# First pair of blocks loaded singly, x by tokens loaded last, and another rate for loads in the order's model

## The chip, the cores and the metric

One core of one Trainium2 chip runs the kernel. The metric is the device time of one execution in microseconds (us). TensorE (PE) multiplies, VectorE (DVE), ScalarE (ACT) and GpSimd (POOL) work on tiles, and SyncE (SP) issues nearly all DMAs, in one queue.

## The reference

Two decoder layers on 512 tokens of width 1024, f32. `concat` is over the two mixers.

```python
def hybrid_layer(h, p_i, layer_idx, norm_gain, w_in, w_out, ...):
    u = rmsnorm(h, norm_gain) @ w_in
    qa, ka, va, ga, qd, kd, vd, gd = jnp.split(u, list(np.cumsum(IN_SPLITS)[:-1]), axis=-1)
    ...
    y = jnp.concatenate([oa * jax.nn.silu(ga), od * jax.nn.silu(gd)], axis=-1) @ w_out
    h = h + y
    gate = jax.nn.sigmoid(rmsnorm(h, ple_norm_gain) @ w_ple_gate)
    return h + (p_i @ w_ple) * gate
```

`oa` is a dilated window attention over 8 heads, `od` a differential attention over 4 heads. A last RMSNorm follows.

## The kernel before

**Products.** Each f32 operand is split into a high part, rounded to fp32r by ACT, and a low part, the rest, made by DVE or POOL. A product is three passes over the same block of 128 rows of depth: high by high, high by low weights, low by high weights (`PASSES`). Weights come in pairs of blocks of 128x512 (512 KB): one DMA fills a staging buffer (`stg`, or `of` for the fourth pair), ACT writes the high part of both blocks into `ring`, DVE and POOL write the low part of one block each. `ring` has five places for pairs. The input x comes transposed (`xt`, four DMAs of two blocks of 128 channels) into `fr`; ACT and DVE split it with the norm's gain (`gt`) into `xy`.

**The start.** PE first runs `NWARM` matmuls on zeros into one bank (`b<-pt`). The first chunk of products (the values `vd` of layer 0) is made by rows: `units_by_rows` goes over four pairs r of blocks of depth, and for each over the four token tiles t, six matmuls each (two blocks, three passes), into four banks `b_79` to `b_82`. So 96 matmuls of 128x512 stand there (`b<-ring,xy`), and behind them the next chunk's (`b<-xy,ring`). The norm's factor is not in these products; it is applied when a bank is emptied. It comes from x by tokens (`x2`, four DMAs of 512 KB into `fr` and `of`): ACT and DVE sum squares (`x_sumsq`), DVE adds (`rstd`), and POOL takes a power for each of four token tiles (`st<-st 128x1`). `spread` then makes PE transpose the four factors (`b<-idt,st`), ACT copies the result to `cr`, and DVE multiplies the rotary tables by it.

**What sets the order.** Nothing is issued as the code stands. Every operation is recorded with a due place (`plan.at`, `plan.pe`, helper `st`), and `Machine.schedule` replays the records through a model of the engines with a duration for each (`cost`), the loads in one stream at a rate in bytes per us, with at most eight loads in flight; what could run first by this model, and among those what is wanted first, stands first in its engine's order. The chip's engines then each keep that order. All recorded instructions come from one line, 292 (`replay`), so they are told apart by their tiles.

The due places of the first loads:

```python
        st(-8.5, load_gt)
        for r in range(4):
            st(-6 + 0.1 * r, load_xt, r)
        ...
        for t in range(T):
            st(3.0 + 0.3 * t, load_x, t)
            ...
            st(3.2 + 0.3 * t, rstd, t, RS0)
```

Of the kernel before, what the change touches and what calls it, by code (L numbers as in the profile page):

```python
# [11 lines left out]
AF = mybir.ActivationFunctionType  # L12
# [45 lines left out]
class Plan:  # L58
# [7 lines left out]
    def pe(self, t, us, f, *a):  # L66
        self.pieces.append((t, len(self.pieces), us, f, a))

    def at(self, t, us, f, *a):
        self.items.append((t, us, f, a))  # L70
# [16 lines left out]
class Machine:  # L87
# [100 lines left out]
    def schedule(self):  # L188
        log = self.log

        nodes, at_call = [], {}
        for i, x in enumerate(log):
            k = x[6] if x[0] == "PE" else None
            if k is not None and k in at_call:
                nodes[at_call[k]].append(i)
            else:
                if k is not None:
                    at_call[k] = len(nodes)
                nodes.append([i])
        N = len(nodes)  # L200
        eng = [log[n[0]][0] for n in nodes]
        busy, done = [0.0] * N, [None] * N
        for i, n in enumerate(nodes):
            for j in n:
                b, d = self.cost(*log[j][:4])
                done[i] = d if isinstance(d, tuple) else busy[i] + d
                busy[i] += b
        preds, seen = [None] * N, {}
        for i, n in enumerate(nodes):
            dep = set()  # L210
            for j in n:
                todo = self.accesses(log[j])
                for k, m, w in todo:
                    for p, mp, wp in seen.get(k, ()):
                        if (w or wp) and mp & m:
                            dep.add(p)
                for k, m, w in todo:
                    lst = seen.setdefault(k, [])
                    if w:
                        lst[:] = [(p, mp & ~m, wp) for p, mp, wp in lst if mp & ~m]  # L220
                    lst.append((i, m, w))
            dep.discard(i)
            preds[i] = sorted(dep)
        succ = [[] for _ in range(N)]
        for i, ps in enumerate(preds):
            for p in ps:
                succ[p].append(i)

        clock, want = START, [None] * N
        for i in range(N):  # L230
            if eng[i] == "PE":
                want[i] = clock
                clock += busy[i]
        end = clock + 10.0

        def lag(i):
            c = done[i]
            return c[0] + 2.0 + c[1] / 200e3 if isinstance(c, tuple) else c
        for i in range(N - 1, -1, -1):
            w = want[i] if want[i] is not None else end  # L240
            for s in succ[i]:
                w = min(w, want[s] - lag(i) - (MARGIN if eng[s] == "PE" and eng[i] != "PE" else 0.0))
            want[i] = w

        left = [len(p) for p in preds]
        ready_at = [0.0] * N
        free = dict.fromkeys(self.eng, 0.0)
        dma, landed = 0.0, []
        waiting = {e: [] for e in self.eng}
        for i in range(N):  # L250
            if not left[i]:
                waiting[eng[i]].append(i)
        order = []
        for _ in range(N):
            best = None
            for e, lst in waiting.items():
                if not lst:
                    continue
                t = max(free[e], min(ready_at[i] for i in lst))
                if best is None or t < best[0]:  # L260
                    best = (t, e)
            t, e = best
            i = min((i for i in waiting[e] if ready_at[i] <= t + 1e-9), key=lambda i: (want[i], i))
            waiting[e].remove(i)
            order.append((t, len(order), i))
            free[e] = t + busy[i]
            if isinstance(done[i], tuple):

                t = max([t] + landed[-8:-7])
                free[e] = t + busy[i]  # L270
                dma = max(dma, t + 1.4) + done[i][1] / 230e3
                fin = dma + 0.6
                landed.append(fin)
            else:
                fin = t + done[i]
            for s in succ[i]:
                if eng[s] == "PE":

                    r = t + busy[i] if e == "PE" else fin + MARGIN
                else:  # L280
                    r = fin
                ready_at[s] = max(ready_at[s], r)
                left[s] -= 1
                if not left[s]:
                    waiting[eng[s]].append(s)
        self.model = (max(free.values()), order, nodes, eng, busy, preds)
        return [j for _, _, i in order for j in nodes[i]]
# [33 lines left out]
def trunk(tc, x, p, w_in, w_out, w_gate, w_ple, final_gain, tables, xt, gt, lams, sub, out):  # L321
# [4 lines left out]
    ACT, DVE, POOL, SPQ, PE = (M.proxy(e) for e in ("ACT", "DVE", "POOL", "SP", "PE"))  # L326
    mm = PE.matmul

    with tc.tile_pool(name="sb", bufs=1) as sb, tc.tile_pool(name="ps", bufs=1, space=PSUM) as psp, \
# [26 lines left out]
        RS0 = ST[:, 136:140]  # L356
# [5 lines left out]
        FRB = FR.rearrange("p (b n) -> p b n", n=512)  # L362
# [16 lines left out]
        def UT(reg, lo, kb):  # L379
            return XY[reg][:, (8 * lo + kb) * 512:(8 * lo + kb + 1) * 512]  # L380
# [14 lines left out]
        plan = Plan()  # L395
        at, pe = plan.at, plan.pe
        nbank = [0]
        NWARM = 14

        def bank():  # L400
            nbank[0] += 1
            return BANK[2 + (nbank[0] - 1) % 6]
# [10 lines left out]
        def stage(n):  # L413

            return OF[:, 4:6, :] if n == NSTG else STG[:, (n - (n > NSTG)) % NSTG]

        def emit_loads():
            order = sorted(range(len(loads)), key=lambda i: loads[i][:2])
            for n, i in enumerate(order):
                t, us, src, hi, lo, eng = loads[i]  # L420
                st = stage(n)

                def load(st=st, src=src):
                    SPQ.dma_start(st, src)

                def high(st=st, hi=hi):
                    ACT.activation(hi, st, AF.Copy)

                def low(k, st=st, hi=hi, lo=lo, eng=eng):
                    eng[k].tensor_sub(lo[:, k], st[:, k], hi[:, k])  # L430
                if n <= NSTG:
                    at(-10, 54.05 + 0.1 * n, load)
                else:
                    prev = loads[order[n - NSTG - (n < 2 * NSTG + 1)]]
                    at(prev[0], prev[1] + 3.5, load)
                at(t, us, high)
                for k in range(2):
                    at(t, us + 1.0 + 0.5 * k, low, k)
# [42 lines left out]
        def units_by_rows(s0, w, ureg, dones):  # L481
            o = [BANK[0], BANK[1], bank(), bank()]

            def part(r, t):
                for kb in (2 * r, 2 * r + 1):
                    for n, (ul, wl) in enumerate(PASSES):
                        mm(o[t], UT(ureg, ul, kb)[:, t * 128:(t + 1) * 128], w(wl, kb),
                           start=(kb == 0 and n == 0), stop=(kb == KB - 1 and n == 2))
            for r in range(4):
                for t in range(T):  # L490
                    pe(s0 + r + 0.25 * t, 1.362, part, r, t)
            for t in range(T):
                dones[t](s0 + 3.2 + 0.25 * t, o[t])

# [31 lines left out]
        def spread(tt, rs, rot):  # L526
            b = {}

            def tr():
                b[0] = bank()  # L530
                for t in range(T):
                    PE.transpose(b[0][:, t * 128:(t + 1) * 128], rs[:, t:t + 1].to_broadcast([128, 128]), IDT)

            def f():
                ACT.activation(RB, b[0], AF.Copy)
                if rot:
                    DVE.tensor_mul(C0, C, b[0])
                    DVE.tensor_mul(SN0, SN, b[0])
            pe(tt, 0.436, tr)
            at(tt, 0.1, f)  # L540
# [30 lines left out]
            SPQ.dma_start(GT, gt)  # L571

        def load_xt(r):
            SPQ.dma_start(FRB[:, 2 * r:2 * r + 2, :], xt[:, 2 * r:2 * r + 2, :])

        def xt_hi(kb):
            ACT.activation(UT(0, 0, kb), FRB[:, kb, :], AF.Copy, scale=GT[:, kb:kb + 1])
# [20 lines left out]
        def warm_up():  # L598
            b = bank()
            for i in range(NWARM):  # L600
                mm(b, PT[:, 0, 0:128], PT[:, 0, 0:512], start=(i == 0), stop=(i == NWARM - 1))

# [23 lines left out]
        def st(us, f, *a):  # L626
            at(-10, 60 + us, f, *a)
# [3 lines left out]
        for r in range(4):  # L631
            st(-6 + 0.1 * r, load_xt, r)
# [8 lines left out]
        for t in range(T):  # L641
# [1 line left out]
            for h in range(2):  # L643
                st(3.1 + 0.3 * t, x_sumsq, t, h)
            st(3.2 + 0.3 * t, rstd, t, RS0)
        spread(2.5, RS0, True)


        nP = [0]
# [536 lines left out]
```

## Time and profile before

| | |
|---|---|
| median of 3 runs | 687.06 us (686.59 to 687.45) |
| the profiled execution | 686.98 us |
| its span, first to last instruction | 684.9 us |
| PE busy | 673.3 us, 98% |
| DVE, ACT, POOL busy | 435.4, 373.8, 383.4 us |

The span is what the trace shows; 2.1 us of the execution lie outside it. A PE that is busy is not idle, but its matmuls may still be slow: their step is read from the distance of their starts.

### The profile page before, as it was taken

How to read it: one execution, taken by the hardware profiler on the slowest of the kernel's cores; microseconds unless marked ns; L12 is line 12 of the kernel's file. 1: busy time of each engine (PE TensorE's matmuls, PEld its weight loads, DVE VectorE, ACT ScalarE, POOL GpSimd, SP SyncE). 2: the span in 40 equal slices, each digit the busy share in tenths (PEclk: the TensorE clock that was granted, in tenths of full speed). 3: DMA queues.
4: the chain of work that ended last, by engine and by line, in shares of the span. 5: the costliest groups of instructions: out<-in, count | busy, mean ns of one | idle time of the engine just before them, and what ended most of it. 6: DMA issues, size and time to landing. Idle time of an engine off the chain costs nothing.

```text
span 684.9 us, 9572 instructions
## 1 busy us (share of the span) xinstructions
PE 673.3 (98%) x3310; PEld 564.0 (82%) x3310; DVE 435.4 (64%) x839; ACT 373.8 (55%) x782; POOL 383.4 (56%) x289
## 2 busy tenths in 40 slices
PE   9999999999999999999999999999999999999995
PEld 7788888888888888888888888888888888788884
DVE  5447996667766784445443699874777688534333
ACT  6525756558888545425432457663787855453411
POOL 5669460876713357937484867266753246496311
PEclk9999999999999999999999999999999999999998
DMA  8656351435443533434152463233535262343002
GB/s 332 242 155 178 93 153 32 140 107 134 119 118 93 184 123 97 138 106 150 62 175 74 123 177 116 78 107 80 154 96 150 92 217 92 98 149 122 1 32 93
DMA packets 31105, 85.32 MB, mean 125 GB/s; under 512 B 4560, under 2 KB 4816, under 8 KB 31056
## 3 DMA queue, kind: packets, MB, share of 16 engines
q1 hardware_dynamic: 30912, 84.44, 39.9%
q8 instruction: 26, 0.43, 0.2%
q10 hardware_dynamic: 144, 0.26, 0.1%
q14 instruction: 23, 0.19, 0.1%
HBM read 63.72 MB, written 4.19 MB: 99 GB/s over the span
## 4 chain that ended last, share of the span: by engine, by line
PE 94%; DVE 3%; DMA 1%; issue 1%; ACT 0%; POOL 0%; SPq 0%; POOLq 0%; DVEq 0%; ACTq 0%
PE b L292 94%; DVE fr L292 2%; DMA gt<-in_gt_dram 1%; DVE misc L292 1%; DVE xy L292 0%; DVE ring L292 0%; ACT xy L292 0%; POOL st L292 0%; DVE of L292 0%; SPq L292 0%; POOL fr L292 0%; DVE st L292 0%; POOLq L1182 0%; ACT of L292 0%; ACT misc L292 0%
## 5 line engine op out<-in xcount | busy, mean ns | idle before, releaser
L292 PE MATMUL b<-xy,ring 128*128 128x512 f32 x1728 | 419.0, 393 | 0.2
L292 PEld LDWEIGHTS b<-xy,ring 128*128 128x128 f32 x1728 | 318.5, 188 | 63.7 <-DVE fr L292 1.9
L292 POOL TENSOR_TENSOR ring<-stg,ring 128x512 fp32r<-128x512 f32 x164 | 233.8, 1451 | 162.7 <-ACT ring L292 131.9
L292 PE MATMUL b<-ring,xy 128*128 128x512 f32 (+1 forms) x600 | 141.6, 385 | 1.5 <-ACT xy L292 1.3
L292 ACT ACTIVATE ring<-stg 128x1024 fp32r<-128x1024 f32 x95 | 100.0, 1059 | 51.2 <-PE b L292 33.5
L292 PEld LDWEIGHTS b<-ring,xy 128*128 128x128 f32 x600 | 107.4, 188 | 23.3 <-ACT xy L292 1.8
L292 ACT ACTIVATE fr<-fr,st 128x512 f32<-128x512 f32 (+3 forms) x193 | 101.8, 556 | 36.8 <-DVE st L292 34.4
L292 POOL TENSOR_TENSOR fr<-fr 128x512 f32<-128x512 f32 x53 | 74.1, 1400 | 30.1 <-ACT fr L292 25.6
L292 POOL TENSOR_TENSOR fr<-fr,cr 128x512 f32<-128x512 f32 x32 | 43.3, 1352 | 63.4 <-DVE fr L292 63.3
L292 DVE CUSTOM_DVE_ANT_0 fr<-b,ct 128x512 f32<-128x512 f32 (+3 forms) x128 | 58.5, 485 | 31.8 <-PE b L292 31.0
L292 DVE SCALAR_TENSOR_TENSOR xy<-fr,gt,xy 128x512 fp32r<-128x512 f32 x32 | 36.6, 1152 | 30.7 <-ACT xy L292 30.7
L292 PE MATMUL b<-qk 128*128 128x128 f32 (+3 forms) x256 | 52.5, 324 | 0.1
L292 DVE TENSOR_TENSOR ring<-stg,ring 128x512 fp32r<-128x512 f32 x26 | 34.6, 1332 | 22.1 <-ACT ring L292 22.1
L292 DVE TENSOR_TENSOR pt<-b,pt 128x384 fp32r<-128x384 f32 (+1 forms) x72 | 40.2, 593 | 11.9 <-ACT pt L292 11.5
L292 ACT ACTIVATE pt<-b 128x384 fp32r<-128x384 f32 (+1 forms) x72 | 34.6, 525 | 18.3 <-PE b L292 18.1
L292 PEld LDWEIGHTS b<-qk 128*128 128x128 f32 x256 | 38.9, 189 | 4.5 <-issue 0.8
L292 PEld LDWEIGHTS b<-idt,fr 128*128 128x128 f32 x284 | 34.0, 140 | 7.3 <-DVE fr L292 0.8
L292 ACT ACTIVATE nt<-fr 128x512 fp32r<-128x512 f32 x32 | 19.8, 624 | 36.6 <-POOL fr L292 36.6
L292 PE MATMUL b<-idt,fr 128*128 128x128 f32 x284 | 39.7, 272 | 0.0
L292 DVE TENSOR_TENSOR fr<-b,cr 128x512 f32<-128x512 f32 x48 | 32.7, 680 | 10.5 <-PE b L292 10.3
L292 POOL TENSOR_TENSOR st<-st 128x4 f32<-128x4 f32 (+1 forms) x19 | 17.8, 938 | 32.8 <-DVE st L292 32.3
L292 ACT ACTIVATE fr<-fr 128x512 f32<-128x512 f32 x26 | 16.4, 633 | 35.1 <-DVE fr L292 34.5
(78 smaller groups left out, 583.0 us busy)
## 6 DMA issues: line engine op xcount, KB each, us to landing
stg<-in_w_in_dram SPq DMA_DIRECT2D x63, 512.0 KB, 3.4
qk<-nt SPq DMA_DIRECT2D x128, 128.0 KB, 2.3
stg<-in_w_out_dram SPq DMA_DIRECT2D x16, 512.0 KB, 4.2
stg<-in_w_ple_gate_dram SPq DMA_DIRECT2D x16, 512.0 KB, 3.3
fr<-in_xt_dram SPq DMA_DIRECT2D x8, 512.0 KB, 5.2
stg<-in_w_ple_dram SPq DMA_DIRECT2D x4, 512.0 KB, 3.2
hsave<-fr SPq DMA_DIRECT2D x8, 256.0 KB, 2.3
fr<-hsave SPq DMA_DIRECT2D x4, 512.0 KB, 3.8
```

The source lines that it names most:

```text
L292: getattr(self.eng[e], op)(*args, **kw)
```

## The change

The first pair of weight blocks (n = 0) is loaded as two DMAs of 256 KB, and its high part is made in two ACT instructions. The first pair of x's blocks is loaded as two DMAs of 256 KB. On PE the first pair of depth is done block by block over the four token tiles: three matmuls each, twelve for block 0, then twelve for block 1. The warm-up has 11 matmuls for 14. The due place of `spread` moves from 2.5 to 3.3. In the model, loads run at 400e3 bytes per us for 230e3, and a load of at most 65,536 bytes is wanted 6.0 us ahead of its use for 2.0.

```diff
-            return c[0] + 2.0 + c[1] / 200e3 if isinstance(c, tuple) else c
+            if isinstance(c, tuple):
+
+                return c[0] + (2.0 if c[1] > 65536 else 6.0) + c[1] / 200e3
+            return c
...
-                dma = max(dma, t + 1.4) + done[i][1] / 230e3
+                dma = max(dma, t + 1.4) + done[i][1] / 400e3
...
-        NWARM = 14
+        NWARM = 11
...
-                def load(st=st, src=src):
-                    SPQ.dma_start(st, src)
-
-                def high(st=st, hi=hi):
-                    ACT.activation(hi, st, AF.Copy)
+                def load(st=st, src=src, ks=((0, 1) if n == 0 else (slice(0, 2),))):
+                    for k in ks:
+                        SPQ.dma_start(st[:, k], src[:, k])
+
+                def high(st=st, hi=hi, ks=((0, 1) if n == 0 else (slice(0, 2),))):
+                    for k in ks:
+                        ACT.activation(hi[:, k], st[:, k], AF.Copy)
...
-            def part(r, t):
-                for kb in (2 * r, 2 * r + 1):
+            def part(kbs, t):
+                for kb in kbs:
...
-                    pe(s0 + r + 0.25 * t, 1.362, part, r, t)
+                    if s0 == 0 and r == 0:
+                        for k in range(2):
+                            pe(0.5 * k + 0.125 * t, 0.681, part, (k,), t)
+                    else:
+                        pe(s0 + r + 0.25 * t, 1.362, part, (2 * r, 2 * r + 1), t)
...
-            SPQ.dma_start(FRB[:, 2 * r:2 * r + 2, :], xt[:, 2 * r:2 * r + 2, :])
+            for k in ((2 * r,), (2 * r + 1,)) if r == 0 else ((2 * r, 2 * r + 1),):
+                SPQ.dma_start(FRB[:, k[0]:k[-1] + 1, :], xt[:, k[0]:k[-1] + 1, :])
...
-        spread(2.5, RS0, True)
+        spread(3.3, RS0, True)
```

The new rate moves rows on all engines. Three places of the new order follow.

SP's queue from the program's first load on. Before:

```order
L292 DMA stg<-in_w_in_dram 128x1024
L292 DMA fr<-in_xt_dram 128x1024
L292 DMA gt<-in_gt_dram 128x32
L292 DMA stg<-in_w_in_dram 128x1024
L292 DMA fr<-in_xt_dram 128x1024
L292 DMA stg<-in_w_in_dram 128x1024
L292 DMA fr<-in_xt_dram 128x1024
L292 DMA fr<-in_x_dram 128x1024 x2
L292 DMA of<-in_x_dram 128x1024 x2
L292 DMA of<-in_w_in_dram 128x1024
L292 DMA fr<-in_xt_dram 128x1024
L292 DMA stg<-in_w_in_dram 128x1024 x3
```

And now, from the first load on:

```order
L295 DMA gt<-in_gt_dram 128x32
L295 DMA fr<-in_xt_dram 128x512
L295 DMA stg<-in_w_in_dram 128x512 x2
L295 DMA fr<-in_xt_dram 128x512
L295 DMA stg<-in_w_in_dram 128x1024
L295 DMA fr<-in_xt_dram 128x1024
L295 DMA stg<-in_w_in_dram 128x1024
L295 DMA fr<-in_xt_dram 128x1024
L295 DMA of<-in_w_in_dram 128x1024
L295 DMA fr<-in_xt_dram 128x1024
L295 DMA fr<-in_x_dram 128x1024 x2
L295 DMA of<-in_x_dram 128x1024 x2
```

The gains' load went from third to first, the blocks of pair 0 are four loads of 128x512, and x by tokens went behind all of the first chunk's weights and `xt`; the second chunk's first load (`stg<-in_w_in_dram 128x1024 x2`) is the row that follows.

PE and ACT around `spread` (`b_86<-idt,st` on PE, `cr<-b_86` on ACT). Before, on PE from the third pair of depth on, and on ACT from the third pair's split on:

```order
L292 MATMUL b_79<-ring,xy_63 128x512 x6
L292 MATMUL b_80<-ring,xy_63 128x512 x6
L292 MATMUL b_81<-ring,xy_63 128x512 x6
L292 MATMUL b_82<-ring,xy_63 128x512 x6
L292 MATMUL b_86<-idt,st 128x128 x4
L292 MATMUL b_79<-ring,xy_63 128x512 x6
L292 MATMUL b_80<-ring,xy_63 128x512 x6
L292 MATMUL b_81<-ring,xy_63 128x512 x6
L292 MATMUL b_82<-ring,xy_63 128x512 x6
```

```order
L292 ACTIVATE xy_63<-fr,gt 128x512 x2
L292 ACTIVATE fr,st<-fr 128x512 x2
L292 ACTIVATE of,st<-of 128x512 x2
L292 ACTIVATE ring<-of 128x1024
L292 ACTIVATE cr<-b_86 128x512
L292 ACTIVATE xy_63<-fr,gt 128x512 x2
```

And now, the same two places:

```order
L295 MATMUL b_79<-ring,xy_63 128x512 x6
L295 MATMUL b_80<-ring,xy_63 128x512 x6
L295 MATMUL b_81<-ring,xy_63 128x512 x6
L295 MATMUL b_82<-ring,xy_63 128x512 x6
L295 MATMUL b_79<-ring,xy_63 128x512 x6
L295 MATMUL b_80<-ring,xy_63 128x512 x6
L295 MATMUL b_81<-ring,xy_63 128x512 x6
L295 MATMUL b_86<-idt,st 128x128 x4
L295 MATMUL b_82<-ring,xy_63 128x512 x6
```

```order
L295 ACTIVATE ring<-of 128x1024
L295 ACTIVATE xy_63<-fr,gt 128x512 x2
L295 ACTIVATE fr,st<-fr 128x512 x2
L295 ACTIVATE of,st<-of 128x512 x2
L295 ACTIVATE ring<-stg 128x1024 x3
L295 ACTIVATE xy_64<-b_79,st 128x4x128
```

The four transposes went from 72 to 90 of the 96 matmuls, and ACT's split of the last two `xt` blocks no longer stands behind the copy to `cr`, which is five rows further down now.

POOL behind its clearing of `qk`, before and now:

```order
L292 MEMSET qk 64x512 x4
L292 TENSOR_TENSOR ring<-stg,ring 128x512 x3
L292 TENSOR_TENSOR st<-st 128x1 x4
L292 TENSOR_TENSOR ring<-of,ring 128x512
L292 TENSOR_TENSOR ring<-stg,ring 128x512 x9
```

```order
L295 MEMSET qk 64x512 x4
L295 TENSOR_TENSOR ring<-stg,ring 128x512 x3
L295 TENSOR_TENSOR ring<-of,ring 128x512
L295 TENSOR_TENSOR ring<-stg,ring 128x512 x2
L295 TENSOR_TENSOR st<-st 128x1 x4
L295 TENSOR_TENSOR ring<-stg,ring 128x512 x7
```

The four powers stood behind three low parts; now they stand behind six, the last two of which (`x2`) belong to the second chunk's first pair, loaded behind x by tokens.

## Rows read from the trace of the kernel before

**Rows 1.** Page, part 1: busy us, share of the span, instructions.

```profile
PE 673.3 (98%) x3310; PEld 564.0 (82%) x3310; DVE 435.4 (64%) x839; ACT 373.8 (55%) x782; POOL 383.4 (56%) x289
```

**Rows 2.** Chain that ended last, around 25 us: start us, us, what.

```profile
25.14 0.72 ACT xy L292
...
25.89 0.76 DVE xy L292
```

**Rows 3.** Timeline, PE, 0 to 45 us: start, us, what, idle before.

```profile
1.45 6.00 PE L292 MATMUL b<-pt 128*128 128x512 f32 x14 [1.45 <-DVE st L292]
7.28 16.89 PE L292 MATMUL b<-ring,xy 128*128 128x512 f32 x72
24.02 0.60 PE L292 MATMUL b<-idt,st 128*128 128x128 f32 x4
25.91 6.08 PE L292 MATMUL b<-ring,xy 128*128 128x512 f32 x24 [1.29 <-ACT xy L292]
31.82 13.46 PE L292 MATMUL b<-xy,ring 128*128 128x512 f32 x57
```

**Rows 4.** Timeline, PE's weight loads, 0 to 45 us.

```profile
8.03 15.73 PEld L292 LDWEIGHTS b<-ring,xy 128*128 128x128 f32 x70 [0.49 <-DVE xy L292]
...
26.70 4.86 PEld L292 LDWEIGHTS b<-ring,xy 128*128 128x128 f32 x22 [0.49 <-DVE xy L292]
```

**Rows 5.** Timeline, PE: the twelfth and fourteenth warm-up apart, and 8.9 to 23.9 us.

```profile
6.30 0.63 PE L292 MATMUL b<-pt 128*128 128x512 f32 x1
...
7.06 0.39 PE L292 MATMUL b<-pt 128*128 128x512 f32 x1
...
8.60 15.58 PE L292 MATMUL b<-ring,xy 128*128 128x512 f32 x68
```

**Rows 6.** Timeline, ACT, 0 to 45 us.

```profile
4.24 1.06 ACT L292 ACTIVATE ring<-stg 128x1024 fp32r<-128x1024 f32 x1 [2.01 <-DMA stg<-in_w_in_dram]
...
8.01 1.06 ACT L292 ACTIVATE ring<-stg 128x1024 fp32r<-128x1024 f32 x1 [0.20 <-DMA stg<-in_w_in_dram]
9.28 1.34 ACT L292 ACTIVATE xy<-fr,gt 128x512 fp32r<-128x512 f32 x2 [0.21 <-DMA fr<-in_xt_dram]
...
18.24 1.06 ACT L292 ACTIVATE ring<-of 128x1024 fp32r<-128x1024 f32 x1 [0.55 <-DMA of<-in_w_in_dram]
24.65 0.60 ACT L292 ACTIVATE cr<-b 128x512 f32<-128x512 f32 x1 [5.35 <-PE b L292]
```

**Rows 7.** Timeline, DVE and then POOL, 0 to 45 us.

```profile
5.33 0.69 DVE L292 TENSOR_TENSOR ring<-stg,ring 128x512 fp32r<-128x512 f32 x1 [3.92 <-ACT ring L292]
7.23 1.41 DVE L292 SCALAR_TENSOR_TENSOR xy<-fr,gt,xy 128x512 fp32r<-128x512 f32 x2 [1.21 <-ACT xy L292]
...
9.15 1.80 POOL L292 TENSOR_TENSOR ring<-stg,ring 128x512 fp32r<-128x512 f32 x1 [1.99 <-ACT ring L292]
...
16.20 3.33 POOL L292 TENSOR_TENSOR st<-st 128x1 f32<-128x1 f32 x4 [2.89 <-DVE st L292]
...
27.50 7.78 POOL L292 TENSOR_TENSOR ring<-stg,ring 128x512 fp32r<-128x512 f32 x6 [6.32 <-PE b L292]
```

**Rows 8.** Loads issued at 1.17, 10.63, 15.67, 16.95: KB each, us to landing.

```profile
fr<-in_xt_dram SPq DMA_DIRECT2D x1, 512.0 KB, 4.9
...
stg<-in_w_in_dram SPq DMA_DIRECT2D x1, 512.0 KB, 10.1
...
ct<-in_tables_dram SPq DMA_DIRECT2D x1, 512.0 KB, 11.5
...
misc<-in_lams_dram SPq DMA_DIRECT2D x1, 256.0 KB, 10.9
```

**Rows 9.** Windows: stretch, length, busy of engines, granted clock, DMA share, GB/s.

```profile
5.00:6.00 1.00, 1.00 (x4) 0.78 (x3) 0.67 (x1) 0.29 (x1) 0.56 (x1) 1.00 0.48 144
```

**Rows 10.** Windows, same columns (PE, PEld, DVE, ACT, POOL): two later stretches.

```profile
32.00:675.00 643.00, 642.36 (x3183) 539.56 (x3183) 415.87 (x800) 353.14 (x751) 364.76 (x266) 1.00 0.39 117
60.00:95.00 35.00, 34.77 (x185) 29.01 (x184) 32.86 (x68) 21.17 (x59) 23.54 (x18) 1.00 0.50 136
```

## The prediction

> **What bounds the kernel now.** I read the page's first part: PE is busy for 673.3 of 684.9 us [rows 1]. So time can only come from three places: PE's idle stretches, its matmuls at a slow pace, and its tail. Then a long window: from 32 to 675 us PE is busy for 642.36 of 643 us [rows 10], so nearly all that can be saved lies before 32 us. There I read PE's timeline. Warm-ups run from 1.45 us, the first real matmul starts at 7.28, the 96 real ones and four transposes follow, and the next chunk starts at 31.82 [rows 3].
>
> The step of a matmul comes from starts. 68 stand between 8.60 [rows 5] and the transposes at 24.02 [rows 3]: 15.42 / 68 = 0.2268 us. That is near 512 columns at 2.4 GHz. The warm-ups are slower: the first starts at 1.45, the twelfth at 6.30, some 0.43 us a step, which is 512 columns at 1.2 GHz. The fourteenth starts at 7.06 and the first real one only 0.22 later [rows 3, 5], so the pace rose at about 6.9 us. The granted clock reads 1.00 already before that [rows 9]; I go by the pace.
>
> Without waits the stretch from 7.28 would take 96 x 0.2268 + 0.60 = 22.37 us, so the next chunk would start at 29.65. It starts at 31.82: 2.17 us are lost. The reader sees where. At 8.03 the weight load has waited 0.49 us for a low part of x [rows 4]. At 25.91 PE has idled 1.29 us for ACT [rows 3], and at 26.70 the weight load 0.49 for DVE [rows 4]. ACT's timeline tells why: its copy to `cr` waited until the transposes were done (24.65), and the last split of x stands behind it [rows 6], high part at 25.14, low part at 25.89 [rows 2]. The data had long been there.
>
> **The change part by part.**
>
> *Three warm-ups fewer.* The twelfth matmul on PE becomes a real one: it starts at 6.30, where the twelfth warm-up starts now [rows 5]. Real ones take the places of warm-ups 12, 13 and 14, two of them still at the slow pace, so by 7.28 three are done: gain 3 x 0.2268 = 0.68 us, if the data is there at 6.30. Is it? The gains, x's block 0 and weight block 0 are 16 + 256 + 256 KB, about one of the old blocks, and the first old block was copied from 4.24 [rows 6]. Then ACT needs about 0.6 (half a pair at 1.06) and DVE 0.69 [rows 6, 7]: about 5.6 us, with 0.7 to spare. Block 1 is needed twelve matmuls in, at 7.28 + 9 x 0.2268 = 9.32. It has landed by about 6.4 (1040 KB, and the second old block landed at 1.17 + 4.9 = 6.1 [rows 8]); 0.7 for ACT and 0.75 for DVE give about 7.9, and POOL's low part, at most 1.80 [rows 7], is done before that too. The next pair is needed at 12.04; the fourth old block was split from 9.28 [rows 6], so its low parts are done by about 11.5. I cost the two extra DMAs and the extra ACT instruction at nothing: SP and ACT wait for loads there. If that cover is gone, each of them is below 0.6 us.
>
> *Half blocks.* What one costs in a full queue: a block of 512 KB issued at 15.67 landed 11.5 later, at 27.2, and the 256 KB issued next at 16.95 landed at 27.85 [rows 8], 0.65 us after it. Whole blocks come at (18.24 - 8.01) / 8 = 1.28 us each [rows 6]. So a half costs half; I take nothing for the split. Upper bound: a half as long as a whole block, 4 x 0.64 = 2.56 us for four. The Trainium skill (DMA: Bandwidth & Descriptors, Anatomy of one DMA) gives 2.0 us plus bytes / 436e3 for a transfer, in a path issued by GpSimd; if that held one after another, two more transfers would cost 4 us, an estimate from that page. The trace's 0.65 us for 256 KB on SP's queue speaks against it.
>
> *`spread` moved, ACT's order.* The wait of 1.29 and its second part go, since the last split of x no longer stands behind the copy. With the early 0.49 this is the 2.17 us above. Together with 0.68 the next chunk would start at 31.82 - 2.85 = 28.97.
>
> *x by tokens last, POOL's order.* This gives something back. PE reaches the transposes after 90 real matmuls: 7.28 + 87 x 0.2268 = 27.01 us. They need all four of POOL's powers, and these stand behind the low parts of the second chunk's first pair, whose load stands behind x by tokens. Ahead of it are twelve blocks of 512 KB and the gains, the same as before the thirteenth block today. That one landed at 10.63 + 10.1 = 20.73 [rows 8]. ACT's high part takes 1.06 [rows 6], to 21.8. Two low parts of POOL at 7.78 / 6 = 1.30 [rows 7] give 24.4, and four powers 3.33 [rows 7] give 27.75; with handing over 27.8. So PE waits 27.8 - 27.0 = 0.8 us at the transposes, where nothing waited for POOL before. Queued behind them is only the last token tile's six matmuls and the next chunk. The banks are emptied in that time, which hides the emptying: its factor needs the first power, at 25.3.
>
> Bounds of this wait: the loads lose time early. Between the copies at 4.24 and 8.01 two blocks and the gains landed, 3.77 us for 2.56 [rows 6], and only 144 GB/s moved from 5 to 6 us [rows 9]. Without these 1.21 us the powers end at 26.6 and PE waits 0. Above: two low parts at 1.80 [rows 7] add 1.0, half blocks as long as whole ones 2.56: a wait of 4.4. I take 0.8, since nothing in the trace says that the slow stretch goes with the gains' place. The Trainium skill (DMA: Bandwidth & Descriptors, Specifications) puts rows under 512 B below line rate; the gains have 128 B a row and stand inside that stretch, but at the head of the queue they would delay everything behind them alike.
>
> *The rate in the model.* It alters rows all over, with the same work. I cost it at nothing: the cover is the loads, which have landed well before use, and PE, idle for 0.64 us in 643 [rows 10]. What it could cost is a rival.
>
> **Sum.** 686.98 - 0.68 - 2.17 + 0.8 = 684.93, against the profiled execution, which is 0.08 below the median of the runs: 684.9 us.
>
> **The rivals.**
>
> *No wait for the powers:* if the loads lose no 1.21 us early, PE's 2.85 us are kept: 684.1. For it: the loss is not in the steady stretch. Against: its cause isn't seen.
>
> *Given back in the new order:* DVE is busy for 32.86 of 35 us from 60 to 95 us [rows 10], so a row that comes late there makes PE wait. If each of the two layers got PE's idle time of the long stretch once more, 2 x 0.64 = 1.3 us, the time is 686.2. Against: PE hardly waits there now, and all of that work starts earlier with PE.
>
> *The low pace stays longer:* if the first half blocks come 1.2 us later and cost as much as whole ones, block 0 is ready at about 7.4 us, PE idles for over 0.6 us after its warm-ups, and the level may rise only after the twelve matmuls of block 0: 12 x 0.2 = 2.4 us more. That is 3.1 us, and the wait for the powers then hides under it: 686.98 - 2.85 + 3.1 = 687.2. The trace shows only one rise, after 5.5 us of unbroken work.
>
> *Slower, late powers:* the same place as in my sum, at the upper bound of 4.4 us for 0.8: 686.98 - 2.85 + 4.4 = 688.5. It decides from a fourth power that ends after 31.2 us, since 2.85 + 1.37 = 4.2 us of waiting make the kernel slower by over 0.2%. Against: the half block's 0.65 us.
>
> **How the numbers follow.** My forecast has 0.42, no wait 0.30, given back 0.14, low pace 0.07, slower 0.07. About 0.2% (1.37 us) is what a measurement can tell from no change: the first two are faster (0.72), given back and low pace are within (0.21), the last is slower (0.07). The range takes in the first three, 0.86: from 683.7, a little under the 684.1, to 686.4, a little over the 686.2. The likeliest case alone holds 684.1 to 685.6.
>
> **What would show it.** Right: the first `b<-ring,xy` on PE at about 6.3 us; no idle on ACT before a `cr` copy with x's split behind it; PE idle for about 0.8 us before `b<-idt,st` at 27 us, ended by POOL; the next chunk at about 29.8. Wrong: a load time above 21.5 us for the thirteenth block, a second slow stretch of matmuls, or new idle time on PE behind 32 us, above all from 60 to 95 and at the same place of the second layer.

## The result

The changed kernel takes 692.36 us, the median of five runs (691.86 to 694.01), for 687.06 before: a ratio of 1.0082 with a 95% interval from 1.007 to 1.0093. I had forecast 684.9 us and a faster kernel; it is 5.3 us slower, outside the range. The profiled execution took 692.35 us with a span of 690.2.

The page's first part of the kernel after, and two windows (stretch, length, busy of PE, PEld, DVE, ACT and POOL, granted clock, DMA share, GB/s):

```profile
PE 674.1 (98%) x3307; PEld 563.1 (82%) x3307; DVE 435.1 (63%) x839; ACT 372.7 (54%) x783; POOL 383.3 (56%) x289
```

```profile
32.00:675.00 643.00, 636.91 (x3137) 533.43 (x3136) 411.88 (x792) 350.48 (x748) 364.96 (x264) 1.00 0.39 116
60.00:95.00 35.00, 34.04 (x182) 28.64 (x181) 32.41 (x67) 20.53 (x57) 23.02 (x17) 1.00 0.50 136
```

PE's sum of busy time hardly moved, and that misleads: the span grew by 5.3 us. The long window tells more, because it shows how much of a fixed stretch PE was idle. PE idled for 0.64 us of 643 before [rows 10] and idles for 6.09 now. So 5.45 us are lost where I had forecast nothing, and the rest is at the start. PE's timeline after, 0 to 48 us (start, us, what, idle before), and its weight loads:

```profile
1.45 5.06 PE L295 MATMUL b<-pt 128*128 128x512 f32 x11 [1.45 <-DVE st L295]
6.30 7.02 PE L295 MATMUL b<-ring,xy 128*128 128x512 f32 x26
13.52 14.85 PE L295 MATMUL b<-ring,xy 128*128 128x512 f32 x64 [0.20 <-DVE xy L295]
28.21 0.82 PE L295 MATMUL b<-idt,st 128*128 128x128 f32 x4
28.79 1.64 PE L295 MATMUL b<-ring,xy 128*128 128x512 f32 x6
31.36 16.85 PE L295 MATMUL b<-xy,ring 128*128 128x512 f32 x73 [0.93 <-DVE xy L295]
```

```profile
9.50 0.30 PEld L295 LDWEIGHTS b<-ring,xy 128*128 128x128 f32 x2 [0.30 <-ACT xy L295]
10.29 2.61 PEld L295 LDWEIGHTS b<-ring,xy 128*128 128x128 f32 x12 [0.49 <-DVE xy L295]
13.52 14.43 PEld L295 LDWEIGHTS b<-ring,xy 128*128 128x128 f32 x64 [0.62 <-DVE xy L295]
...
28.70 0.13 PEld L295 LDWEIGHTS b<-idt,st 128*128 128x128 f32 x1 [0.25 <-POOL st L295]
```

The first real matmul starts at 6.30 us, as forecast. Then the weight loads wait at 9.50, 10.29 and 13.52 for the second half block and the second pair of x. ACT's split of that half block (first row) began only at 8.72, when its load was there; POOL's four powers (second row) end at 28.66:

```profile
8.72 0.72 ACT L295 ACTIVATE xy<-fr,gt 128x512 fp32r<-128x512 f32 x1 [1.87 <-DMA fr<-in_xt_dram]
...
26.55 2.11 POOL L295 TENSOR_TENSOR st<-st 128x1 f32<-128x1 f32 x4
```

The 27th real matmul, which without waits would start at 7.28 + 23 x 0.2268 = 12.50, starts at 13.52. The last power delays PE's weight load by only 0.25 us. The next chunk starts at 31.36, for 31.82 before [rows 3] and 29.8 forecast: behind the transposes stand six matmuls, done by 28.79 + 6 x 0.2268 = 30.15, and then PE loses 1.2 us to DVE. DVE's timeline shows what it was doing (the same columns):

```profile
22.53 0.57 DVE L295 TENSOR_SCALAR st<-st 128x1 f32<-128x1 f32 x4
29.42 0.77 DVE L295 TENSOR_TENSOR misc<-misc 128x256 f32<-128x256 f32 x1 [6.32 <-DMA misc<-in_lams_dram]
30.11 0.14 DVE L295 TENSOR_SCALAR st<-st 128x1 f32<-128x1 f32 x1
30.22 0.42 DVE L295 TENSOR_REDUCE st<-misc 128x4 f32<-128x256 f32 x1
30.56 0.74 DVE L295 SCALAR_TENSOR_TENSOR xy<-b,st,xy 128x512 fp32r<-128x512 f32 x1
```

`xy<-b,st,xy` empties the first bank, and PE's next chunk needs that bank. In DVE's order three instructions on two small loads (`lams` and `sub`, scalars and a gain of the differential attention, first used much later) now stand ahead of it, and DVE stood idle for 6.3 us until the load of `lams` landed at 29.4. Before, they stood behind all four emptyings. The order of the changed kernel on DVE there:

```order
L295 TENSOR_SCALAR st<-st 128x1 x4
L295 TENSOR_TENSOR misc<-misc 128x256
L295 TENSOR_SCALAR st<-st 128x1
L295 TENSOR_REDUCE st<-misc 128x4
L295 SCALAR_TENSOR_TENSOR xy_64<-b_79,st,xy_64 128x4x128
```

For the time behind 32 us I read what PE waited for over the whole execution (us in total, times, longest):

```profile
PE b L295 <- DMA qk<-nt: 3.8, 4, 1.2
PE b L295 <- DVE st L295: 1.4, 1, 1.4
PE b L295 <- DVE fr L295: 1.3, 1, 1.3
PE b L295 <- DVE xy L295: 1.1, 2, 0.9
PE b L295 <- DVE ring L295: 0.6, 1, 0.6
```

Only the second row was there before (it is the start of the warm-ups). The first is the largest: `qk<-nt` are copies of 128 KB from one on-chip tile to another, issued on SP's queue, and the attention's scores (`b<-qk`) need them. One of the four places in PE's timeline:

```profile
59.70 7.87 PE L295 MATMUL b<-xy,ring 128*128 128x512 f32 x34
68.52 1.51 PE L295 MATMUL b<-qk 128*128 128x128 f32 x8 [0.96 <-DMA qk<-nt]
```

The four lie at 68.52, 105.16, 402.81 and 439.74 us, the same two in each layer. Counted over PE's whole order, those scores stood behind 249, 348, 1401 and 1500 matmuls on weight blocks before; now they stand behind 243, 342, 1395 and 1494. So six matmuls each, 6 x 0.2268 = 1.36 us of work, went from ahead of the scores to behind them. The issues around the first place (KB each, us to landing; issued at 60.85, 61.54 and 62.16, and two at 63.36 and 63.96):

```profile
qk<-nt SPq DMA_DIRECT2D x1, 128.0 KB, 2.3
...
stg<-in_w_in_dram SPq DMA_DIRECT2D x1, 512.0 KB, 4.5
...
qk<-nt SPq DMA_DIRECT2D x1, 128.0 KB, 4.4
...
qk<-nt SPq DMA_DIRECT2D x2, 128.0 KB, 4.3
```

In this execution a move lands 2.2 to 2.3 us after its issue when no load is ahead of it and 4.1 to 4.5 behind one; at the same place behind the same load it took 3.8 to 4.0 before the change, and 2.9 to 3.4 in e2 below. I put these issue times into the model's formula (rate, 1.4 us ahead, 0.6 behind): at 400e3 the moves issued at 63.96 and 64.60 land at 66.29 and 66.93, at 230e3 at 68.10 and 68.67. The trace has them at 68.27 and 68.73. So the rate that suits the first loads (1.28 us for 512 KB in a full queue) lets these moves land 2 us early in the model, and the planner puts their readers too early. The spacing says the same: behind the load the moves land 0.5 to 0.8 us apart, where 230e3 prices one at 0.57 and 400e3 at 0.33.

### The profile page after: what moved, and what is told of

Read it like the earlier page. It is cut to its first block, busy times and chain, and to the rows that moved or that the text cites. A ratio compares the mean times of both kernels' runs of the same rounds, so it can differ in the third digit from the quotient of the medians.

```text
span 690.2 us, 9561 instructions
## 1 busy us (share of the span) xinstructions
PE 674.1 (98%) x3307; PEld 563.1 (82%) x3307; DVE 435.1 (63%) x839; ACT 372.7 (54%) x783; POOL 383.3 (56%) x289
## 4 chain that ended last, share of the span: by engine, by line
PE 76%; DVE 10%; DMA 7%; issue 2%; ACT 2%; POOL 2%; SPq 1%; POOLq 0%; DVEq 0%; ACTq 0%
PE b L295 76%; DVE fr L295 4%; DMA qk<-nt 3%; DVE misc L295 2%; DMA fr<-in_x_dram 1%; DMA misc<-in_lams_dram 1%; DVE xy L295 1%; SPq L295 1%; DMA fr<-in_xt_dram 1%; ACT fr L295 1%; POOL fr L295 1%; DVE of L295 1%; DVE pt L295 1%; DVE ring L295 1%; DVE nt L295 1%
## 5 line engine op out<-in xcount | busy, mean ns | idle before, releaser
L295 ACT ACTIVATE ring<-stg 128x1024 fp32r<-128x1024 f32 (+1 forms) x96 | 100.0, 1048 | 57.3 <-PE b L295 29.0
L295 PEld LDWEIGHTS b<-ring,xy 128*128 128x128 f32 x600 | 107.6, 189 | 22.4 <-DVE ring L295 1.2
L295 ACT ACTIVATE fr<-fr,st 128x512 f32<-128x512 f32 (+3 forms) x193 | 101.8, 555 | 31.8 <-DVE st L295 29.4
L295 POOL TENSOR_TENSOR fr<-fr 128x512 f32<-128x512 f32 x53 | 75.8, 1431 | 33.1 <-ACT fr L295 30.7
L295 DVE TENSOR_TENSOR ring<-stg,ring 128x512 fp32r<-128x512 f32 x26 | 31.2, 1200 | 22.9 <-ACT ring L295 22.8
L295 DVE TENSOR_TENSOR qk<-fr,nt 64x512 fp32r<-64x512 f32 x32 | 27.0, 844 | 12.9 <-ACT nt L295 12.4
L295 ACT ACTIVATE of<-b,st 128x512 f32<-128x512 f32 (+1 forms) x17 | 11.3, 663 | 40.5 <-PE b L295 35.2
```

Of the source, the lines that this page charges most:

```text
L295: getattr(self.eng[e], op)(*args, **kw)
```

## The experiments

Every kernel is the one before or the changed one with the lines shown. Ratios are to the kernel before on the same chip (its medians: 686.89 to 687.02).

**e1, the rate alone; e2, everything but the rate.** They divide the change in two. In the kernel before, and in the changed one:

```diff
-                dma = max(dma, t + 1.4) + done[i][1] / 230e3
+                dma = max(dma, t + 1.4) + done[i][1] / 400e3
```

```diff
-                dma = max(dma, t + 1.4) + done[i][1] / 400e3
+                dma = max(dma, t + 1.4) + done[i][1] / 230e3
```

> The kernel before with 400e3 for 230e3 in the model and nothing else. Theory (the rate: the model lands the 128 KB moves of q and k too early, so scores on PE stand 3 to 6 matmuls earlier and PE waits for the moves): PE waits for qk<-nt near 68, 105, 402 and 439 us as in the changed kernel, and the time is 691.5 to 694. Rival (the new start puts PE out of step with DVE and SP, the order later is harmless): 686.5 to 687.5, no wait for qk<-nt on PE.

> The changed kernel with 230e3 in the model. Theory (the rate): no PE wait for qk<-nt, the start's gain of 0.5 to 1.5 us is kept to the end: 685.5 to 686.7. Rival (the new start): the waits for qk<-nt stay and the time is 690.5 to 693.

e1 took 690.12 us, ratio 1.0051 (1.0036 to 1.0066): slower by 3.2, not by the 4.5 to 7 that I expected. The four scores stand behind 243, 342, 1395 and 1494 matmuls as in the changed kernel, and PE waits at three of them. What PE waited for, first and third row:

```profile
PE b L292 <- DMA qk<-nt: 2.4, 3, 1.0
...
PE b L292 <- DVE ring L292: 1.3, 2, 0.7
```

e2 took 683.64 us, ratio 0.9951 (0.9936 to 0.9966), with no wait for `qk<-nt`; that is 1.9 us below the range of either theory. Its timeline of PE:

```profile
28.99 2.88 PE L295 MATMUL b<-xy,ring 128*128 128x512 f32 x12
31.71 0.60 PE L295 MATMUL b<-idt,st 128*128 128x128 f32 x4
...
59.88 8.33 PE L295 MATMUL b<-xy,ring 128*128 128x512 f32 x36
68.05 0.49 PE L295 MATMUL b<-idt,fr 128*128 128x128 f32 x3
68.29 1.52 PE L295 MATMUL b<-qk 128*128 128x128 f32 x8
```

So the edits without the rate are worth 3.2 us by the medians, and the one constant loses 3.2 alone and 8.7 on top of them. At the old rate the order also puts the four transposes behind 108 matmuls, not 90, so that nothing waits for the powers; and the three instructions on `lams` and `sub` stand behind the emptyings. e2 beats both kernels.

Not all of the 3.2 us is read at the start. PE's last group of matmuls, before and in e2:

```profile
672.27 4.47 PE L292 MATMUL b<-ring,xy 128*128 128x256 f32 x36
```

```profile
670.15 4.47 PE L295 MATMUL b<-ring,xy 128*128 128x256 f32 x36
```

It ends at 676.74 before and at 674.62 in e2, 2.1 us earlier. The rest is behind it: from there to the end of the span it is 8.2 us before and 7.1 in e2. In the other profiled executions that stretch took 7.0 to 7.7 us. No run changed it alone.

**e3, e4: which transfers the rate misplaces.** e3 is the changed kernel, e4 the one before, with two rates:

```diff
-                dma = max(dma, t + 1.4) + done[i][1] / 400e3
+                dma = max(dma, t + 1.4) + done[i][1] / (400e3 if done[i][1] > 131072 else 230e3)
```

```diff
-                dma = max(dma, t + 1.4) + done[i][1] / 230e3
+                dma = max(dma, t + 1.4) + done[i][1] / (230e3 if done[i][1] > 131072 else 400e3)
```

> The changed kernel with 400e3 in the model for loads over 131072 bytes and 230e3 for the rest. Theory (the rate of the moves does it): as without the new rate or a little above, 685.5 to 688; scores stand 0 to 3 matmuls earlier than before, not 6. If it is the rate of the loads: 690 to 693, with the waits for qk<-nt. Rival (the new start): 690.5 to 693 too.

> The kernel before with 400e3 in the model for transfers of at most 131072 bytes and 230e3 for loads. Theory (the rate of the moves): slower than before, 688.5 to 693, by waits for qk<-nt. If it is the loads' rate or the new start: 686.5 to 687.5.

e3 took 686.86 us, ratio 1.0001 (0.999 to 1.0012): the old rate for the moves alone gives back 5.5 us. Its scores stand three matmuls earlier than before, PE still waits 0.9 us for moves, at two places, and 0.9 us for the first bank. e4 took 689.77, ratio 1.005 (1.0031 to 1.007): the new rate for the moves alone costs 2.9, nearly the 3.2 of e1. I expected e4 to lose it by waits for the moves. In its execution only 0.3 us of PE's waits end with a move; 2.1 us end with DVE's `fr`, at two places. So a misplaced move seems to cost also through what is placed around it; how it does so was not tried.

**e7, e11: the moves told to be late.** The rate stays at 400e3, and only the moves land 2.0 us later in the model, as the trace has them. e7 is the changed kernel; e11 is the one before with the rate and this line:

```diff
-                fin = dma + 0.6
+                fin = dma + (2.6 if log[nodes[i][0]][4][0].name.startswith('qk') and done[i][1] == 131072 else 0.6)
```

> The changed kernel; the model lands the 128 KB moves of q and k 2.0 us later, the rate stays at 400e3. Theory (PE's scores stood too early because the model landed the moves too early): no PE wait for qk<-nt; what is left of the loss is the start's (about 2.4 us against the changed kernel at 230e3): 685.5 to 688. Rival (the loads' rate itself, by other rows): 689.5 to 692.

> The kernel before with 400e3 for 230e3, and the moves of q and k landing 2.0 us later in the model. Theory (the rate costs by the moves alone): the 3.2 us of the rate are won back, 686 to 687.3. Rival: 688.5 to 690.

e7 took 686.12 us, ratio 0.999 (0.998 to 1.0001), 6.2 us less than the changed kernel. PE's waits in it:

```profile
PE b L295 <- DVE st L295: 1.4, 1, 1.4
PE b L295 <- DVE xy L295: 0.9, 1, 0.9
PE b L295 <- DVE ring L295: 0.4, 1, 0.4
PE b L295 <- ACT xy L295: 0.2, 1, 0.2
```

The waits for the moves are gone, and the one for the emptied bank (`xy`, 0.9) is left. e11 took 686.3, ratio 0.9987 (0.9974 to 0.9999): all of the rate's 3.2 us is won back. In both the order differs elsewhere too, since other rows follow the moves.

**e5, e9: the load of `lams`.** In the model, DMAs into `misc` land 20 us later, so that DVE's order has their readers behind. e5 is the changed kernel with this line; e9 has both this delay and e7's:

```diff
-                fin = dma + 0.6
+                fin = dma + (20.6 if log[nodes[i][0]][4][0].name.startswith('misc') else 0.6)
```

> The changed kernel; the model lands the load of the lambdas (misc) 20 us later, which moves only DVE's lambda instructions behind the emptying of the first chunk's banks. Theory (DVE stands still for misc<-in_lams to 29.4 us, and the emptying of bank 0 behind it holds back the next chunk): the next chunk starts at 29.8 to 30.2 for 31.36, and the time is 690.4 to 691.4. Rival (the late loads and powers set the next chunk's start): it stays at 31.0 to 31.4, the time at 692.

> The changed kernel with both corrections in the model: the moves of q and k land 2.0 us later, the lambdas' load 20 us later; the rate stays at 400e3. Theory (these two landings are the loss): the gains of 6.2 and 2.0 us add up, 683.7 to 684.9, as good as the old rate. Rival (they hide each other, or something else of the rate costs): 685.5 to 687.

e5 took 690.34 us, ratio 1.0049 (1.0034 to 1.0064), 2.0 less than the changed kernel; in its profiled execution (691.13) the next chunk starts at 30.57, not at 29.8 to 30.2. DVE's timeline has the reason:

```profile
29.65 0.21 DVE L295 TENSOR_SCALAR st<-st 128x1 f32<-128x1 f32 x2 [7.26 <-DMA st<-in_sub_dram]
29.78 1.40 DVE L295 SCALAR_TENSOR_TENSOR xy<-b,st,xy 128x512 fp32r<-128x512 f32 x2
```

The next small load, `sub`, had taken the place of `lams` in front of the emptying. It stands there in e9 too, but in that execution it had landed by 28.68, an emptying takes 0.7, and PE came to the bank at 28.57 + 6 x 0.2268 = 29.93:

```profile
28.57 1.62 PE L295 MATMUL b<-ring,xy 128*128 128x512 f32 x6
30.03 3.34 PE L295 MATMUL b<-xy,ring 128*128 128x512 f32 x14
```

e9 took 684.93 us, ratio 0.9974 (0.9965 to 0.9984): 7.4 less than the changed kernel, and 1.2 less than e7, as much as PE lost at 30.15. (e5's 2.0 holds more than that: PE waits for a move three times in it, not four.) The waits for the moves and for the bank are both absent from e9.

**e10: `spread` alone.** The kernel before with `spread(3.3, RS0, True)` for `spread(2.5, RS0, True)`.

> The kernel before with the due place of spread at 3.3 and nothing else (the order puts x by tokens behind xt by this alone). Theory (the wait of 1.29 us at 25.9 with its second part is worth 1.5 to 1.9): 685.2 to 685.7. Rival (powers and emptied banks come late instead): 686.5 to 687.5.

It took 684.92 us, ratio 0.9968 (0.9953 to 0.9984): 2.0 us for one number, a little more than I expected. The order it makes also loads x by tokens behind `xt`, so that this is no edit of its own. The waits at 25.91 and 26.70 [rows 3, 4] are gone:

```profile
7.55 22.00 PE L292 MATMUL b<-ring,xy 128*128 128x512 f32 x96
29.39 2.88 PE L292 MATMUL b<-xy,ring 128*128 128x512 f32 x12
```

**e6, e8: half blocks and warm-ups, in e2.** e6 loads and splits the first pairs whole again; e8 has 14 warm-ups:

```diff
-                def load(st=st, src=src, ks=((0, 1) if n == 0 else (slice(0, 2),))):
+                def load(st=st, src=src, ks=(slice(0, 2),)):
...
-                def high(st=st, hi=hi, ks=((0, 1) if n == 0 else (slice(0, 2),))):
+                def high(st=st, hi=hi, ks=(slice(0, 2),)):
...
-            for k in ((2 * r,), (2 * r + 1,)) if r == 0 else ((2 * r, 2 * r + 1),):
+            for k in ((2 * r, 2 * r + 1),):
```

```diff
-        NWARM = 11
+        NWARM = 14
```

> The changed kernel with 230e3 in the model and the first pairs of weights and x loaded and split as whole pairs again. Theory (half blocks slow the loads, 0.7 to 1 us each for the 0.65 of a full queue): the thirteenth block lands at 20.7 to 21.0 for 22.4, the time is 683.0 to 684.2. Rival (a slow stretch of the first 8 us, whatever the block's size): it lands at 22 to 22.5.

> The changed kernel with 230e3 in the model and 14 warm-ups. Sum of the prediction (three real matmuls in the place of warm-ups): 0.68 us slower than with 11, 684.3. Rival (PE waits for the late half blocks at 10 and 13 us anyway, so the warm-ups stand in waiting time): the same to 0.3 us, 683.5 to 684.0.

e6 took 686.4 us (685.17 to 687.17), ratio 0.9988 (0.9978 to 0.9998): the halves are worth 2.8 us by the medians, 1.6 by the two profiled executions, where I had expected no loss without them. Its first real matmul comes late, after 1.62 us of idle PE, since the first pair of x has to land whole, at 7.3:

```profile
8.12 22.38 PE L295 MATMUL b<-ring,xy 128*128 128x512 f32 x96 [1.62 <-ACT xy L295]
```

Its thirteenth 512 KB were issued at 11.31 and landed 10.2 later, at 21.5, between the two expectations:

```profile
of<-in_x_dram SPq DMA_DIRECT2D x1, 512.0 KB, 10.2
```

In the seven profiled executions with half blocks and the gains' load they landed at 22.4 to 22.9. So, by this one execution of e6, four half blocks for two whole ones cost the loads about 0.9 us. Before, with whole blocks and the gains third in the queue and not first, they landed at 20.8.

e8 took 683.74 us, ratio 0.995 (0.9933 to 0.9966), the same as e2:

```profile
1.45 5.12 PE L295 MATMUL b<-pt 128*128 128x512 f32 x14 [1.45 <-DVE st L295]
6.42 0.50 PE L295 MATMUL b<-ring,xy 128*128 128x512 f32 x1
7.29 21.83 PE L295 MATMUL b<-ring,xy 128*128 128x512 f32 x95 [0.36 <-DVE ring L295]
28.96 2.88 PE L295 MATMUL b<-xy,ring 128*128 128x512 f32 x12
```

Its fourteen warm-ups ran faster than those before [rows 3], so this execution doesn't show what 14 cost at the slower pace; the next chunk starts at 28.96, in e2 at 28.99. Nor does it show the rival's reason: the second half block of x landed at 7.0 here, for 8.2 in e2, and PE's weight loads did not wait at 10 and 13 us.

**e12: no load of the gains, in e2.**

```diff
-            SPQ.dma_start(GT, gt)
+            POOL.memset(GT, 1.0)
```

> This is the changed kernel with the model's old rate (as e2), and without the gains' load: GpSimd fills the gains' tile with ones instead (the true gains are left out), every other row of the order stays. Two theories on the slow loads of the first nine microseconds. If the gains' transfer with its 128 bytes a row takes the bandwidth there, the blocks behind it land as they do later, 0.65 us for a half block and 1.28 us for a whole one, and the thirteenth block of 512 KB lands 0.7 us or more earlier than the 22.43 us of e2, at 21.7 or before. If the loads are slow at the start whatever stands first in the queue, the blocks still land about 1.0 us apart for a half, and the thirteenth comes within 0.4 us of 22.43. The time stays at 683.3 to 684.0 us by both, since TensorE hardly waits for a load in e2.

It took 683.66 us, ratio 0.9952 (0.9935 to 0.9969), the same as e2. Its next chunk starts at 28.01, 1.0 us earlier than e2's, but of the 643 us from 32 on PE is idle for 1.86, in e2 for 1.06. The thirteenth 512 KB, issued at 10.97, landed 10.2 us later (first fence), at 21.19, where e2's, issued at 12.20, landed at 22.43. The window from 5 to 6 us is no faster than before (second fence, 119 GB/s, for 144 [rows 9]):

```profile
of<-in_x_dram SPq DMA_DIRECT2D x1, 512.0 KB, 10.2
```

```profile
5.00:6.00 1.00, 1.00 (x5) 0.79 (x3) 1.00 (x2) 0.99 (x2) 0.00 (x0) 1.00 0.32 119
```

So the load of 16 KB of gains at the queue's head cost the loads 1.2 us in this pair of executions, and something else makes the stretch at 5 us slow. Of the 1.2 us, 0.44 are SP's place for it: without it the first load is issued at 0.73, with it at 1.17. The Trainium skill (DMA: Bandwidth & Descriptors, Specifications) puts transfers under 512 B below line rate. The gains have 128 B a row, and the other 0.8 us would agree with that, but no run loads 16 KB in longer rows, and five executions with the changed kernel's order of loads differ by 0.4 in the same landing.

## Why the prediction was wrong

**The step that failed: "The rate in the model ... I cost it at nothing: the cover is the loads, which have landed well before use".** The loads are not the only transfers that this line prices. The moves `qk<-nt` are used when they land, and no cover stands behind them. The rival "given back in the new order" named 60 to 95 us and the same of the second layer, where two of the four waits lie (68.52 and 402.81; 105.16 and 439.74 lie behind). But its mechanism was a late row on DVE, and it sized the loss by PE's old idle time, at 1.3 us. Shown: four scores stand six matmuls too early and wait 3.8 us for the moves; e7, which corrects the moves in the model and nothing else, gives back 6.2 of the 8.7 us that lie between the changed kernel and e2.

**A second step failed: "The banks are emptied in that time, which hides the emptying".** I looked at the factor that the emptying needs and not at what stands ahead of it on DVE. PE lost 1.2 us there. e9 against e7 shows it, at 1.2 us.

The two account for 7.4 of the 8.7 us. Of the 1.3 left between e9 and e2, 1.04 stand at the next chunk's start (30.03 and 28.99). In e9 the transposes still stand ahead of the last six matmuls, which is 28.57 - 28.11 = 0.46 by its timeline, but e2 has them to do later, at 31.71. A weight load at 6.64 waits 0.43 for DVE in e9, which in e2 none does; this is read, not tried.

**Right.** The waits at 25.91 and 26.70 go with `spread`: e10 gains 2.0 us, where the sum had 2.17 with the early 0.49 in it. The first real matmul starts at 6.30.

**Right by luck.** At the old rate the next chunk starts at 28.99, where I had 28.97, and the time is 683.64, where "no wait for the powers" had 684.1. But my 28.97 has the four transposes in front, and e2 makes them later, where they take 0.36 (31.71 to 32.07); set against like, its start is 0.4 us late. And part of its gain lies behind PE's last matmul, where I had forecast none.

**Mis-sized.** The three warm-ups, 0.68 us in the sum, show as 0.1 between e8 and e2. In the changed kernel the second half block of x lands at 8.70 and not at 6.4, and PE waits for it and for the next pair; whether this is why the warm-ups are worth so little is not shown. The wait for the powers, 0.8 in the sum, is 0.25: the powers end at 28.7 for 27.75, but PE itself comes 1.0 us late. The thirteenth 512 KB landed at 12.78 + 10.1 = 22.9 us, beyond the 21.5 that I had named as a sign against me. I had taken nothing for the split into halves, which cost about 0.9 (e6), and had counted the gains alike in either place. Luck hid part of it: the four powers took 2.11 us, where I had 3.33, so that 1.2 of the 2.2 us by which the block came late don't show. The warm-ups' early step is 4.85 / 11 = 0.44 us, not the 0.43 that I wrote; nothing hangs on it.

**By the sum.** Forecast 684.9; the next chunk is 31.36 - 29.8 = 1.56 us late, and PE's idle time behind 32 us grew by 5.45: 691.9 of the 692.35 measured in that execution. The sum is nearer than its parts: PE's last matmul ends at 682.83, 6.1 us later than before, of which the start and the idle time give 5.0, and the stretch behind it is 0.8 shorter.

**Open.** Why the loads are slow from 5 to 7 us in every kernel, the old one included; and the rest of PE's losses in the changed kernel that no move ends, such as 1.3 us at 582 us behind DVE's `fr`. They are gone in e9, but no run changed them alone. So it stays open how the 6.2 us that e7 gives back come about beyond the 3.8 that are waits for moves. It is open too why the stretch behind PE's last matmul was longer in the profiled execution of the kernel before.

## What to carry to other kernels

A constant in a planner's model prices every instruction that uses it: before changing a DMA rate to suit one kind of transfer, list the others and compare each kind's modelled landing with the trace. When loads or due places move, read each in-order engine's new rows around them for a small load's reader that now stands ahead of something urgent; its use may be far away, its wait is not. And undo such a constant by itself: here the other edits together are a gain of 3.2 us that it hid.

## What the hardware showed that I had not expected

A copy of 128 KB between on-chip tiles lands 2.2 to 2.3 us after its issue when no load is ahead of it and 2.9 to 4.5 behind a 512 KB load in the same queue, though 512 KB pass in 1.28 us when the queue is full of loads. PE's faster pace (2.4 GHz for 1.2) comes at different times in different executions: fourteen warm-ups took 6.00 us before [rows 3] and 5.12 in e8, with the granted clock reading 1.00 throughout. Two 512 KB loads issued as four halves at the head of the queue put later loads back by about 0.9 us (e6 against e2), though a half took 0.65 in a full queue. And in the one pair of executions compared, a load of 16 KB in rows of 128 B at the head of the queue cost 1.2 us, about as much as 512 KB.
